# Another order by hand for layer 1 of an NSA / mLSTM step: emissions 3 to 6

## The chip, the core and the metric

The kernel runs on one core of a Trainium2 chip. The core has five engines that each take their own instructions in order: PE (the matrix unit; PEld is its weight load), DVE (vector), ACT (scalar, with the activation functions), POOL (GpSimd) and SP, which here only issues DMAs. They meet through semaphores. The metric is the device time of one execution in microseconds, the median of several runs.

## The reference

One inference step of a trunk of two layers, `x <- x + Mixer(RMSNorm(x))`, over 512 prompt tokens and 8 sample tokens, 520 columns in all, with model width 1024. Layer 0 is sparse attention (compressed, selected and window branches). Layer 1 is an mLSTM with 4 heads of width 512, and a final RMSNorm follows. Beside the outputs y the step returns the new cache rows and the new states. What matters here is layer 0's last matmul and layer 1:

```
out0  = (o * silu(z0)) @ w_out0 ;  x1 = x + out0           # 1024 x 1024
proj  = rmsnorm(x1) @ w_in                                  # 1024 -> xm 2048 | z 2048
c     = silu(conv_b + sum_j xpad[:, j:j+T] * conv_w[j])     # causal, width 4
q, k  = block-diagonal 4x4 of c ;  v = block-diagonal of xm
ig, fl = gates of concat(q, k, v) @ w_gate + b_gate
# prompt, per head: D = cumulated gates (causal), S = (q k^T) * exp(D - m)
num   = S v + decay * (q C) ; den = sum S + decay * (q n) ; h = num / max(|den|, exp(-m))
C     = carry * C + sum_s k_s w_s v_s^T                     # 512 x 512 per head
# samples: the same with one token and their own C, n, m: 8 x 4 matrices of 512 x 512
out   = (rmsnorm(h) * norm_w + skip * c) * silu(z) ;  y = x1 + out @ w_out
```

All in float32. The kernel forms a float32 product from rounded parts: an operand is split in a high half (`hhi`, `whi`, `uh`, ...: a copy in the type fp32r) and a low half (`hlo`, `wlo`, `ul`, ...: operand minus high half), and three matmuls high x high, high x low and low x high are added up.

## The kernel before, in words

Channels lie on the 128 partitions and tokens on the free axis; the 520 columns are two halves c = 0, 1 of 260. A weight tile of 128 x 1024 is loaded (`wraw`), its high half is made by a copy (`whi`, on ACT or DVE) and its low half by a subtraction (`wlo`, on DVE or POOL). Each half of an output tile takes 8 x 3 = 24 matmuls of 260 columns.

The order of the work is written out by hand. The program first records: with the recorder on, each engine call goes through `Engine.__getattr__` (line 507 issues it in the end, which is why all rows of the profile say L507) and becomes a piece of a list (`Rec`, lines 426 to 478), or an operation of a plan with its dependences (`Plan`, lines 324 to 360). Then the pieces are emitted in an order that a tuple of numbers gives, seven times:

- emissions 0 to 2 (`CALLS0`, `CALLS2`, `ORDER0`): layer 0's compression and projections, and the attention
- emission 3 (`CALLS1`, line 1956; 712 pieces, about 459 to 643.5 us): layer 0's output projection by tiles `out.ft.c` (8 tiles, 2 halves) with the addition to `x` (`x1`), the splits into `hhi` and `hlo` and the sums of squares (`sacc`, closed by a matmul with ones and the chain `rs_y`, `rv`, `rs_t`, `rr`); then layer 1's projections `xm.ft.c` of 16 tiles, convolution (`cva`), silu (`cvs`, `CT`), values (`VT`), gate products (`QKS`, `VS`) and the gates
- emission 4 (`ORDER1`, line 2312; 348 operations, to 748.3 us): the z projections of layer 1 (`zt`, `zsg`), the gates of the prompt, and head 0's state steps for the samples (`cs` in, `cs` out, 512 KB each)
- emission 5 (`ORDER2`, line 2709; 933 operations, to 997 us): for each of the 4 heads the splits of the values (`vh`, `vl`), the scores and keys (`f_po`, `f_pk`, `f_s`, `f_c`), the values (`num`), the state steps of the other heads, and the output unit with its weights (`uh`, `ul`, `x<-x,mm`)
- emission 6 (`CALLS3`, line 2760): the last part of the output, the final norm and late cache rows

The program schedules nothing of its own, so each engine's stream is its pieces in the order of the list, and the instruction at the head of a stream that waits for a semaphore holds what is behind it. SP issues its DMAs in the same way. Tiles of rotating buffers are taken in the order of the list too: a load into a buffer waits for the last reader of what was there. The `MOVED` tuples that go with the lists swap the engine of single pieces (`swapped`, lines 481 to 490): a copy by ACT goes to DVE, a copy by DVE to ACT, and a subtraction, product, addition or scalar operation from DVE to POOL or back.

Of the kernel before, what the change touches and what calls it, by code (L numbers as in the profile page):

```python
# [123 lines left out]
)  # L124
ORDER2 = (
# [42 lines left out]
)  # L168
CALLS0 = (
# [122 lines left out]
MOVED3 = (  # L292
    2, 12, 16, 23, 30, 31, 35, 42, 65, 69, 103, 120, 124, 136, 141,
)
# [249 lines left out]
def step_kernel(ctx, tc, ap):  # L544
# [1410 lines left out]
    xm_val(15)  # L1955
    R.run(NE, CALLS1, MOVED1)
    mctx.close()
# [912 lines left out]
```

## Time and profile before

| | us |
|---|---|
| median of 3 runs (lowest, highest) | 1036.99 (1036.32, 1039.83) |
| profiled execution | 1041.29 |
| its span in the trace | 1039.6 |
| PE busy in the span | 1016.4 |
| DVE, ACT, POOL busy | 790.0, 553.2, 321.7 |
| granted clock, mean | 0.995 |

The profile is of one execution. Its rows name an instruction by engine, operation and tiles (`out<-in`, buffer numbers left out), so `mm<-hhi,wlo` is a matmul of the activations' high half with a weight's low half. PE's matmuls overlap in the rows: the time that one takes is seen from start to next start (0.12 us for 260 columns in a run of them). A bracket at the end of a row gives the idle time of the engine ahead of it and what released it.

### The profile page before, as it was taken

The page shows a single profiled execution, that of the slowest core. Times are in us where ns is not written, and L with a number is a line of the kernel's source. Part 1 is how long each engine was busy: PE and PEld are TensorE (multiplying, and loading weights), DVE is VectorE, ACT ScalarE, POOL GpSimd, SP SyncE. Part 2 cuts the span into 40 slices and gives each one's busy share as a digit, 9 for nine tenths or more (in the row PEclk, how much of TensorE's full clock was granted, in tenths as well). Part 3 has the DMA queues.
Part 4 walks back from the last instruction along what each step waited for, and adds up shares of the span by engine and source line. Part 5 has one row for each costly group of instructions (what it writes and reads, how often), then busy time and mean ns, then how long its engine had stood idle before and what let it go on. Part 6 is the DMA issues. An engine that isn't in the chain of part 4 may idle for free.

```text
span 1039.6 us, 23563 instructions
## 1 busy us (share of the span) xinstructions
PE 1016.4 (98%) x8743; PEld 909.5 (87%) x8743; DVE 790.0 (76%) x1903; ACT 553.2 (53%) x1260; POOL 321.7 (31%) x374
## 2 busy tenths in 40 slices
PE   7999999999999999999999999999899999999998
PEld 6999999999998878789999998899766678877897
DVE  7856756586579988964878786775698989888985
ACT  5454344622388788632445444766455564634543
POOL 1233423331232434423331332232332234242330
PEclk9999999999999999999999999999899999999999
DMA  7654644144526344655645253788778698988543
GB/s 256 194 176 156 194 123 130 47 125 135 164 68 198 100 127 130 182 179 184 179 148 171 92 184 121 244 277 289 272 267 276 237 346 287 326 288 276 203 123 113
DMA packets 124789, 197.16 MB, mean 190 GB/s; under 512 B 16117, under 2 KB 66166, under 8 KB 124418
## 3 DMA queue, kind: packets, MB, share of 16 engines
q1 hardware_dynamic: 118866, 186.37, 55.1%
q10 hardware_dynamic: 5808, 9.28, 2.5%
q8 instruction: 69, 1.13, 0.5%
q14 instruction: 46, 0.38, 0.1%
HBM read 145.89 MB, written 58.10 MB: 196 GB/s over the span
## 4 chain that ended last, share of the span: by engine, by line
PE 79%; DVE 10%; ACT 4%; DMA 4%; issue 2%; POOL 1%; SPq 0%; DVEq 0%; ACTq 0%; POOLq 0%
PE mm L507 48%; PE s L507 17%; PE t L507 8%; PE d L507 5%; DVE cs L507 2%; ACT zsg L507 1%; DMA wc<-in_w_qkv 1%; DMA x1d<-x 1%; DVE wlo L507 1%; DVE s L507 1%; DVE hx L507 1%; DMA wraw<-in_m_in 1%; DMA praw<-in_cache 1%; ACT s L507 1%; DVE num L507 0%
## 5 line engine op out<-in xcount | busy, mean ns | idle before, releaser
L507 PE MATMUL mm<-hhi,whi 128*128 128x260 f32 (+1 forms) x952 | 273.5, 287 | 0.9 <-ACT VT L507 0.9
L507 PE MATMUL mm<-hhi,wlo 128*128 128x260 f32 (+1 forms) x952 | 270.6, 284 | 0.1
L507 PE MATMUL mm<-hlo,whi 128*128 128x260 f32 (+1 forms) x952 | 270.1, 284 | 0.0
L507 PEld LDWEIGHTS mm<-hhi,whi 128*128 128x128 f32 (+1 forms) x952 | 179.1, 188 | 5.2 <-issue 2.7
L507 PEld LDWEIGHTS mm<-hhi,wlo 128*128 128x128 f32 (+1 forms) x952 | 179.0, 188 | 0.4 <-DVE wlo L507 0.3
L507 PEld LDWEIGHTS mm<-hlo,whi 128*128 128x128 f32 (+1 forms) x952 | 178.5, 187 | 0.7
L507 POOL TENSOR_TENSOR wlo<-wraw,whi 128x1024 fp32r<-128x1024 f32 (+1 forms) x40 | 78.6, 1967 | 122.1 <-ACT whi L507 39.8
L507 ACT ACTIVATE whi<-wraw 128x1024 fp32r<-128x1024 f32 (+1 forms) x65 | 57.0, 881 | 77.0 <-PE mm L507 33.0
L507 DVE SCALAR_TENSOR_TENSOR cs<-t,wk,cs 128x512 f32<-128x512 f32 x128 | 88.7, 740 | 8.9 <-ACT cs L507 8.3
L507 ACT ACTIVATE cs<-cs,SBC 128x1024 f32<-128x1024 f32 x64 | 71.5, 1142 | 26.8 <-PE d L507 19.6
L507 DVE TENSOR_TENSOR wlo<-wraw,whi 128x1024 fp32r<-128x1024 f32 (+2 forms) x62 | 68.8, 1110 | 11.1 <-ACT whi L507 5.8
L507 PE MATMUL s<-phi,w1h 128*128 128x256 f32 (+1 forms) x256 | 75.8, 296 | 0.0
L507 PE MATMUL s<-plo,w1h 128*128 128x256 f32 (+1 forms) x256 | 74.5, 291 | 1.0 <-DVE plo L507 0.9
L507 ACT ACTIVATE s<-s,mn 128x128 f32<-128x128 f32 (+3 forms) x128 | 70.5, 555 | 6.8 <-DVE mn L507 4.8
L507 PE MATMUL s<-phi,w1l 128*128 128x256 f32 (+1 forms) x256 | 74.0, 289 | 0.0
L507 PE MATMUL mm<-uh,whi 128*128 128x260 f32 x224 | 64.5, 288 | 0.6 <-DVE x L507 0.4
L507 PE MATMUL mm<-uh,wlo 128*128 128x260 f32 x224 | 63.6, 284 | 1.1 <-DVE wlo L507 1.1
L507 DVE CUSTOM_DVE_ANT_0 s<-s,D 128x128 f32<-128x128 f32 (+3 forms) x128 | 58.5, 485 | 7.5 <-PE s L507 5.9
L507 PE MATMUL mm<-ul,whi 128*128 128x260 f32 x224 | 63.4, 283 | 0.0
L507 POOL TENSOR_SCALAR s<-s,sm 128x256 f32<-128x256 f32 (+3 forms) x47 | 42.2, 909 | 52.3 <-DVE sm L507 27.6
L507 PEld LDWEIGHTS s<-plo,w1h 128*128 128x128 f32 x256 | 48.4, 189 | 2.2 <-DVE plo L507 1.5
L507 POOL TENSOR_TENSOR plo<-praw,phi 128x1024 fp32r<-128x1024 f32 (+1 forms) x17 | 30.2, 1775 | 63.6 <-DMA praw<-in_cache 29.8
(485 smaller groups left out, 2632.2 us busy)
## 6 DMA issues: line engine op xcount, KB each, us to landing
cs<-in_state_C SPq DMA_DIRECT2D x64, 512.0 KB, 5.5
o_cs<-cs SPq DMA_DIRECT2D x64, 512.0 KB, 5.6
praw<-in_cache SPq DMA_DIRECT2D x128, 128.0 KB, 2.7
dk<-in_cache SPq DMA_DIRECT2D x128, 128.0 KB, 2.7
wraw<-in_m_in SPq DMA_DIRECT2D x32, 512.0 KB, 3.6
wraw<-in_m_out SPq DMA_DIRECT2D x32, 256.0 KB, 5.2
wraw<-in_w_kv SPq DMA_DIRECT2D x11, 512.0 KB, 4.9
wraw<-in_w_q SPq DMA_DIRECT2D x8, 512.0 KB, 3.6
```

The costliest lines, as they stand in the source:

```text
L507: return f(*[real(x) for x in a], **{n: real(x) for n, x in k.items()})
```

## The change

Four of the number tuples are replaced: the orders of emission 3 (`CALLS1`), 4 (`ORDER1`) and 5 (`ORDER2`) with their sets of swapped pieces (`MOVED1`, `MOVEDP1`, `MOVEDP2`). `CALLS3` and `MOVED3`, of emission 6, are written with other line breaks. Emissions 0 to 2 and all code outside the tuples stay as they are. The numbers index the recorded pieces, which are the same. The core of the diff, the first lines of each list (cut):

```diff
@@ ORDER1 @@
-    253, 254, 257, 225, 0, 1, 226, 2, 227, 15, 228, 229, 230, 231, 274, 232, 252, 16, 233, 30, 8, 234, 255, 256, 3,
+    0, 253, 257, 225, 226, 227, 228, 230, 1, 2, 229, 254, 15, 16, 262, 231, 232, 30, 17, 265, 233, 234, 235,
...
@@ ORDER2 @@
-    284, 315, 327, 303, 291, 286, 1, 318, 306, 290, 294, 22, 2, 402, 3, 5, 13, 7, 282, 18, 328, 307, 0, 4, 14, 295,
+    22, 282, 290, 303, 284, 402, 291, 2, 3, 1, 294, 295, 306, 315, 318, 5, 10, 7, 0, 307, 4, 13, 316, 18, 31,
...
@@ CALLS1 @@
-    44, 535, 249, 70, 28, 45, 46, 15, 0, 21, 22, 65, 64, 69, 66, 9, 4, 29, 53, 10, 30, 31, 11, 37, 12, 60, 61, 67,
+    440, 15, 0, 44, 28, 63, 1, 21, 16, 19, 4, 22, 26, 25, 70, 65, 64, 3, 9, 5, 45, 8, 6, 46, 60, 53, 2, 10, 108,
...
-MOVED1 = (
-    27, 43, 46, 52, 69, 71, 79, 86, 89, 95, 104, 105, 117, 126, 127, 147, 156, 157, 167, 169, 184, 195, 197, 212,
+MOVED1 = (20, 27, 29, 30, 36, 45, 52, 61, 62, 69, 71, 72, 73, 79, 88, 89, 95, 104, 112, 117, 126, 127, 152, 157, 164,
...
-MOVEDP1 = (
-    1, 7, 17, 22, 27, 31, 32, 37, 47, 52, 67, 76, 82, 87, 91, 112, 132, 136, 137, 142, 147, 157, 166, 182, 192, 197,
+MOVEDP1 = (7, 27, 31, 42, 46, 47, 61, 77, 82, 87, 91, 112, 117, 127, 132, 136, 162, 166, 167, 172, 177, 181, 182, 192,
...
-MOVEDP2 = (
-    94, 170, 177, 265, 283, 286, 288, 292, 295, 301, 304, 307, 313, 316, 321, 325, 327, 328, 338, 339, 347, 361,
+MOVEDP2 = (82, 94, 170, 177, 189, 265, 272, 284, 285, 286, 288, 292, 295, 309, 338, 346, 357, 362, 373, 387, 388, 389,
...
```

What the numbers mean at the places that the prediction names: in emission 3 the pieces 93 and 131 are the `hlo` splits of input tiles 5 and 7 for half 0 (41st and 42nd on DVE before, 52nd and 53rd after), 142 is the addition of the last output half (45th before, 49th after), 148 is the matmul that sums its squares (20th and 18th on PE), and 174 is the low half of the second xm weight (43rd and 62nd on DVE). In emission 4 operation 2 is the low half of the first z weight (2nd and 4th on DVE, counted from 0), 227 the first gate bias. In emission 5 operations 286 and 288 are value splits (high halves) on DVE, 289 a low half on POOL, and 300 the first product of values and keys, which comes 20th on PE before and 14th after.

More of the change, by code (lines that the diff above doesn't have):

```diff
@@ L246 @@
 CALLS1 = (
[32 rows of a table removed]
-)
-MOVED1 = (
[6 rows of a table removed]
-)
[33 rows of a table added]
+)
+MOVED1 = (20, 27, 29, 30, 36, 45, 52, 61, 62, 69, 71, 72, 73, 79, 88, 89, 95, 104, 112, 117, 126, 127, 152, 157, 164,
[6 rows of a table added]
 MOVED2 = (
@@ L291 @@
 )
-MOVED3 = (
-    2, 12, 16, 23, 30, 31, 35, 42, 65, 69, 103, 120, 124, 136, 141,
-)
+MOVED3 = (2, 12, 16, 23, 30, 31, 35, 42, 65, 69, 103, 120, 124, 136, 141,)
 MOVEDP0 = (
@@ L301 @@
 )
-MOVEDP1 = (
-    1, 7, 17, 22, 27, 31, 32, 37, 47, 52, 67, 76, 82, 87, 91, 112, 132, 136, 137, 142, 147, 157, 166, 182, 192, 197,
-    202, 207, 211, 217, 225, 230, 255,
-)
-MOVEDP2 = (
[5 rows of a table removed]
-)
+MOVEDP1 = (7, 27, 31, 42, 46, 47, 61, 77, 82, 87, 91, 112, 117, 127, 132, 136, 162, 166, 167, 172, 177, 181, 182, 192,
+    196, 197, 202, 211, 212, 248, 255,)
+MOVEDP2 = (82, 94, 170, 177, 189, 265, 272, 284, 285, 286, 288, 292, 295, 309, 338, 346, 357, 362, 373, 387, 388, 389,
[5 rows of a table added]
 LATE = ((3, 1), (3, 2), (3, 3))
```

208 rows, old and new, of tables (CALLS1, CALLS3, MOVED1, MOVEDP2) are left out of this document.

## The prediction

> **What bounds the kernel now.** I read the page's engine table first, then the chain of waits, the stretches of the three emissions whose lists differ, and last the matmul engine's waits.
>
> ```profile
> span 1039.6 us, 23563 instructions
> PE 1016.4 (98%) x8743; PEld 909.5 (87%) x8743; DVE 790.0 (76%) x1903; ACT 553.2 (53%) x1260; POOL 321.7 (31%) x374
> PE 79%; DVE 10%; ACT 4%; DMA 4%; issue 2%; POOL 1%; SPq 0%; DVEq 0%; ACTq 0%; POOLq 0%
> ```
>
> PE is busy 98% of the span and holds 79% of the chain that ended last. The order of PE's own work hardly matters to its length; what matters is whether each operand is there when PE comes to it. The table by stretch (columns: the stretch, then busy time and number of instructions on PE, PEld, DVE, ACT, POOL, the granted clock, the DMA share and GB/s) has emission 3 at 459 to 643.5 us, emission 4 up to 748.3, emission 5 up to 997 and emission 6 behind it:
>
> ```profile
> 459.00:643.50 184.50, 182.17 (x1576) 177.68 (x1572) 130.63 (x282) 82.89 (x181) 58.49 (x72) 0.99 0.47 152
> 643.50:748.30 104.80, 101.87 (x861) 93.74 (x858) 72.80 (x128) 64.92 (x123) 32.30 (x41) 0.99 0.79 271
> 748.30:997.00 248.70, 245.18 (x1729) 186.77 (x1728) 220.26 (x479) 130.02 (x218) 74.83 (x81) 0.99 0.81 274
> ```
>
> PE is idle for 184.50 - 182.17 = 2.33 us, 2.93 us and 3.52 us: 8.8 us in the 538 us that the change touches. The waits of PE over the whole span, and the one place where a wait has an after-effect:
>
> ```profile
> PE t L507 <- DVE pr L507: 2.9, 1, 2.9
> PE mm L507 <- DVE wlo L507: 2.5, 3, 1.4
> ...
> 747.01 0.34 PE L507 MATMUL t<-pr,ones 128*32 128x32 f32 x8 [2.91 <-DVE pr L507]
> 747.28 1.12 PE L507 MATMUL t<-cst,lse 128*128 128x128 f32 x4
> 748.19 5.20 PE L507 MATMUL mm<-CT,bdm 128*128 128x512 f32 x6
> 753.22 0.60 PE L507 MATMUL t<-cst,VS 128*8 128x128 f32 x4
> ...
> 756.18 1.02 PE L507 MATMUL mm<-CT,bdm 128*128 128x512 f32 x2
> ```
>
> After the wait of 2.91 us, six matmuls of 512 columns took about 5.1 us from start to next start (748.19 to 753.22), 0.84 us each; the same matmul at 756.18 goes at 1.02 / 2 = 0.51 at most. So that wait costs its 2.9 us and 2 us more (6 x 0.33). A list that fed PE without a gap could win 8.8 + 2 = 10.8 us at the very most; what a worse one can lose has no such limit.
>
> **The change, part by part.** The diff replaces the order of emission 3 (712 recorded pieces), of emission 4 (348) and of emission 5 (933), and the sets of instructions whose engine is swapped there. List 6 holds the same numbers in the same order before and after, with other line breaks: its stretch changes by nothing of its own. No instruction is added or removed in the other three; counted in the two lists, 3 to 6% of the pairs on each of PE, DVE and ACT stand the other way round, up to 17% on POOL and on SP, the DMA queue. In emission 3, 45 instructions go from DVE to POOL and 35 back, 33 from ACT to DVE and 28 back. In emission 5 it is 46 and 27, and 22 and 24. So PE's sum of work stays, and the cost is the sum of the places where an operand comes late. I followed the new lists by hand at the borders of the stages, where buffers and engines have least lead, with durations of the trace.
>
> *Start of emission 3.* One of the three waits for a weight's low half is here:
>
> ```profile
> 461.59 0.35 SPq L507 DMA_DIRECT2D scr<-in_state_conv  x1
> ...
> 473.89 1.77 DVE L507 TENSOR_TENSOR wlo<-wraw,whi 128x1024 fp32r<-128x1024 f32 x1
> ...
> 475.71 0.39 PE L507 MATMUL mm<-uo,wlo 128*128 128x260 f32 x1 [1.40 <-DVE wlo L507]
> ```
>
> The SP queue opens at 461.59, when the buffers of the stage ahead come free. The new list puts the weights of output tile 2 earlier behind that point, so the 1.40 us should go; but the weights of tile 3, issued ahead of the block in the old list, now stand behind it, and ahead of the later loads stands a store of x1 that waits for a DVE addition. Term: -1.4, with +2.0 as the other end (the DVE step of 1.77 us, late a second time). I take -1.4, since tile 3 is asked for one tile (2 x 2.9 us of PE) later.
>
> *From the output tiles to layer 1's projection.* Here the list moves most:
>
> ```profile
> 507.64 0.47 PE L507 MATMUL mm<-hhi,whi 128*128 128x260 f32 x1
> ...
> 509.76 0.28 PE L507 MATMUL mm<-hlo,whi 128*128 128x260 f32 x1
> ...
> 510.48 0.28 PE L507 MATMUL mm<-hlo,whi 128*128 128x260 f32 x1
> ```
>
> ```profile
> 506.26 2.08 DVE L507 SCALAR_TENSOR_TENSOR hlo<-x,nw,hhi 128x260 fp32r<-128x260 f32 x5
> 508.69 1.23 DVE L507 TENSOR_TENSOR wlo<-wraw,whi 128x1024 fp32r<-128x1024 f32 x1 [0.34 <-ACT whi L507]
> ...
> 510.73 0.41 DVE L507 TENSOR_TENSOR x<-x,mm 128x260 f32<-128x260 f32 x1
> ```
>
> PE starts the first layer-1 projection at 507.64 and takes the low halves of input tiles 0 to 7 in turn, three matmuls apart: tile 5 at 509.76 and tile 7 at 510.48. In the old list the five splits at 506.26 made the last of these just ahead of PE. In the new one the splits of tiles 5 and 7 follow the addition of the last output half (the row at 510.73) and two other splits. PE finished that half at about 507.4 (the projection follows it without a gap), so the addition lies between 507.9 and, where it lay in before, 510.73; tile 7's split ends 0.41 + 4 x 0.42 = 2.1 us after its start, at 510.0 to 512.8. The second sum of squares, which the new list puts on PE right behind this projection (before, two projections later), needs one more addition of 0.42 us on the same engine and shares the wait. Ends: 0 and 512.8 - 510.48 = 2.3; since the work set ahead of the addition on DVE grows by 3.0 us (counted from the lists with the durations of before), up to 5.3. I take **+2.0**: DVE was 3 us behind here already.
>
> The low half of the next weight (508.69, 1.23 us) falls behind eight further DVE steps, some 3.4 us, the last of which scales the first projection's result. That gives 510.0 + 0.4 + 3.4 + 1.2 = 515.0 to 517.8, plus whatever the chain through ACT's square root adds, about 0.8 in before. PE has two projections and the small sum ahead of it: 507.6 + 2.9 + 0.6 + 2.9 = 514.0, plus the wait just taken. Term **+1.4** (0 to 2.9, one projection).
>
> *Start of emission 4.* The next low half in line is behind more on DVE:
>
> ```profile
> 645.04 1.99 PE L507 MATMUL t<-gs,cst 128*128 128x260 f32 x8
> ...
> 647.11 0.28 PE L507 MATMUL mm<-hhi,wlo 128*128 128x260 f32 x1
> ```
>
> ```profile
> 644.02 1.22 DVE L507 TENSOR_TENSOR wlo<-wraw,whi 128x1024 fp32r<-128x1024 f32 x1
> 645.78 0.49 DVE L507 TENSOR_SCALAR gi<-t,bg 128x260 f32<-128x260 f32 x1 [0.53 <-PE t L507]
> ```
>
> The new list puts it behind the first gate bias, which needs the matmuls at 645.04, and behind a copy that comes over from ACT (0.4): 645.78 + 0.49 + 0.4 + 1.22 = 647.9 where PE asks at 647.11, 0.8 late; the matmul that feeds the bias is moved 0.6 us ahead, which leaves 0.2. Term **+0.5** (0 to 1.0). The low halves of the next two tiles go to POOL, which has nothing there, and PE asks for them 10 us and more later: nothing, and 1 us each if POOL were busy.
>
> *End of emission 4.* The chain to the 2.91 us wait keeps its members and nearly its places: 0.
>
> *Start of emission 5.*
>
> ```profile
> 750.61 0.28 DVE L507 TENSOR_TENSOR bdm<-cst,mw 128x128 f32<-128x128 f32 x1
> ...
> 756.74 0.29 DVE L507 TENSOR_TENSOR bdk<-cst,wc 128x128 f32<-128x128 f32 x1
> ...
> 758.88 1.22 DVE L507 TENSOR_TENSOR bdk<-cst,wc 128x128 f32<-128x128 f32 x1
> ```
>
> ```profile
> 758.67 2.56 POOL L507 TENSOR_TENSOR vl<-VT,vh 128x512 fp32r<-128x512 f32 x2 [11.40 <-ACT vh L507]
> ```
>
> ```profile
> 771.14 0.48 PE L507 MATMUL mm<-vh,kwh 128*128 128x512 f32 x1
> ```
>
> The first values-times-keys product moves on PE from 20.4 to 13.5 us of work behind the start, so it is asked for at 771.14 - 6.9 = 764.2. DVE, free from the head's closing chain at 750.6, has 13.3 us ahead of the last split for it, then POOL one of 1.28: 765.2. Term **+1.0** (-1.0 to +3.0; below nothing if the half-clock matmuls come away).
>
> *The swaps and the other places.* What a swap costs in length, emission 5, POOL then DVE (busy us, mean ns of one, then idle time before):
>
> ```profile
> L507 POOL TENSOR_TENSOR wlo<-wraw,whi 128x512 fp32r<-128x512 f32 x12 | 16.0, 1331 | 36.3 <-PE mm L507 16.0 <-ACT whi L507 11.6 <-DVE whi L507 5.3
> L507 POOL TENSOR_TENSOR ul<-num,uh 128x512 fp32r<-128x512 f32 x7 | 9.9, 1421 | 14.4 <-ACT uh L507 5.8 <-DVE uh L507 4.6 <-PE mm L507 4.0
> ```
>
> ```profile
> L507 DVE TENSOR_TENSOR wlo<-wraw,whi 128x512 fp32r<-128x512 f32 x12 | 8.2, 681 | 0.4 <-ACT rs_y L507 0.4
> L507 DVE TENSOR_TENSOR ul<-num,uh 128x512 fp32r<-128x512 f32 x6 | 4.1, 683 | 0.0
> ```
>
> ```profile
> L507 POOL TENSOR_TENSOR wlo<-wraw,whi 128x1024 fp32r<-128x1024 f32 (+1 forms) x40 | 78.6, 1967 | 122.1 <-ACT whi L507 39.8
> ...
> L507 DVE TENSOR_TENSOR wlo<-wraw,whi 128x1024 fp32r<-128x1024 f32 (+2 forms) x62 | 68.8, 1110 | 11.1 <-ACT whi L507 5.8
> ```
>
> The last two are the whole span's, 40 and 62 low halves of weights. A result made on POOL comes 0.65 to 0.74 us later. In emissions 3 and 5, 45 + 46 = 91 results get this; a move behind one more DVE step costs as much. If one in twelve of the 91 is asked for by PE inside that time, that is 7.6 x 0.7 = 5 us. The rate is my choice: in before 3 of the 102 weight low halves of both engines kept PE waiting, and my five places were found in some 110 of 538 us. Ends: -4.5, the idle time that is left to win (8.8 - 1.4 - 2.9), and +15, the POOL time that emission 5 gains by the lists (a net 19 instructions more, large and small, 0.8 us each on the mean). I take **+5**.
>
> Sum: -1.4 + 2.0 + 1.4 + 0.5 + 1.0 + 5 = **+8.5 us**; the ends add to -6.9 and +29.2. The profiled execution took 1041.29 us, 1.7 more than its span and 4.3 more than the median of 1036.99 (runs 1036.32 to 1039.83), so it would come to about 1049.8, and the median to 1036.99 + 8.5, about **1045**.
>
> **A rule weighed.** The last DVE rows above show one DVE product of 0.29 us taking 1.22 beside POOL's two of 1.28: DVE loses 0.93 us to 1.28 of POOL. The Trainium skill ("SBUF — State Buffer", Who interferes with whom) has a rule for this: a DVE instruction with two SBUF inputs and a POOL instruction that reads SBUF exclude each other, and the later one waits for the whole instruction. The trace agrees at this place. By the rule the relief of DVE in the next part would be eaten up, as the POOL time added blocks DVE in its turn, and the faster rival would shrink to the 1.4 us of the first wait; by the rows of single instructions alone it stands.
>
> **The rivals.** *No measurable change.* PE's leads are long inside the stages (DVE is idle 248.7 - 220.3 = 28 us in emission 5, 54 in emission 3), so the places I found merge and the rest costs nothing: -1.4 + 2.0 + 1.4 = +2, time 1039. Against it: three borders come short by hand at once.
>
> *Much slower.* The waits chain: DVE gets a step that waits for POOL, everything behind it on DVE stands, and PE's pauses reach the length of the one at 747, after which the next 5 us run at half speed. Four such pauses at 2.9 + 2 us are +20, with the sum above +28: time 1065. For it, DVE has hardly a gap behind the start of emission 5 (third figure of the row):
>
> ```profile
> 760.00:780.00 20.00, 19.94 (x141) 13.65 (x139) 19.07 (x37) 10.18 (x18) 6.79 (x10) 1.00 0.76 247
> ```
>
> Against it: only one pause of that length in 538 us of before.
>
> *Faster.* In emission 5 DVE loses 19 instructions net to POOL, at 0.6 us each 11 us of 220. If DVE's backlog is what causes the small waits of PE, they go along with the 1.40 at 475: -1.4 - 4.5 = -6, time 1031. It decides only if nothing at the borders comes late; against it stands that PE's whole idle time in emission 5 is 3.5 us.
>
> *The change does less than it says.* For list 6 this is so, by the diff; for the other three the places differ.
>
> **How the numbers follow.** Chances: the forecast (4 to 18 us slower) 0.62, much slower 0.17, no measurable change 0.13, faster 0.08. A measurement of this kernel tells 0.3% (3.1 us) from no change: slower 0.79, within it 0.13, faster 0.08. The range takes the unmeasurable case's lower edge, 1035, and on the other side most of the much slower case, 1063; the forecast's own range is 1041 to 1055.
>
> **What would show it.** Right: PE's busy time stays near 1016 and its idle time grows by 8 us; the wait at 475 for a low half is gone; a wait of PE for hlo or sacc of about 2 us shows where the first layer-1 projection begins, another for a low half some 8 us on, one of under a microsecond at the gates' start; in emission 5 waits for values made on POOL (ul, vl, wlo). By stretch: +2.0 in emission 3, +0.5 in 4, +1 in 5, and the 5 of the rest mostly in 3 and 5. Wrong: if the three stretches keep 184.5, 104.8 and 248.7 us; if the loss sits in emission 4, where least is swapped; if it comes from DMA waits, which I cost at nothing beyond the start; or if emission 5 becomes shorter, which would mean DVE's load and not its order is what PE waits for.

## The result, and the profile after

The changed kernel takes 1031.48 us (median of 7 runs, 1030.38 to 1033.42) where the kernel before takes 1036.99 (7 runs beside them, 1034.99 to 1039.83): a ratio of 0.9947, 95% interval 0.9930 to 0.9963. So it is 5.5 us faster (3.8 to 7.3), where 8.5 us slower was forecast. The profiled execution took 1030.38 us. From the page of the changed kernel, engines and chain:

```profile
span 1028.6 us, 23534 instructions
PE 1010.4 (98%) x8743; PEld 907.0 (88%) x8743; DVE 780.3 (76%) x1881; ACT 545.7 (53%) x1254; POOL 345.7 (34%) x402
...
PE 88%; DVE 5%; ACT 2%; DMA 2%; issue 1%; POOL 1%; SPq 0%; ACTq 0%; DVEq 0%; POOLq 0%
```

PE does the same 8743 matmuls; its share of the chain rose from 79 to 88%, DVE's fell from 10 to 5. POOL has 24 us more work and DVE 10 us less, as the lists say. Between the two profiles PE's idle time falls from 23.2 to 18.2 us and its busy time from 1016.4 to 1010.4. The busy time of these same matmuls isn't a constant: it is 1012.0 us in the repeated kernel before (below), in part because some matmuls behind a wait go at half speed in one execution and not in another (last section). The stretches of emissions 3, 4 and 5 of the changed kernel (columns as in the table before):

```profile
458.10:638.30 180.20, 179.96 (x1570) 176.01 (x1572) 132.46 (x276) 76.88 (x176) 65.33 (x82) 1.00 0.47 157
638.30:742.20 103.90, 101.73 (x861) 92.76 (x854) 73.26 (x133) 62.75 (x119) 33.58 (x39) 1.00 0.79 277
742.20:986.10 243.90, 241.75 (x1736) 186.81 (x1729) 209.21 (x457) 129.99 (x219) 90.02 (x102) 0.99 0.83 280
```

Against 184.5, 104.8 and 248.7 these are shorter by 4.3, 0.9 and 4.8 us. That is more than the times allow for, because the profile of before was of a long execution (1041.29 us against a median of 1036.99). The stretch of an emission in which nothing was changed, from PE's first matmul of it to the first of the next, is in the profiles of before and of the runs below 181.6 to 184.2 us (mean of 9: 183.0) for emission 3, 104.2 to 104.9 (mean of 10: 104.5) for 4 and 245.0 to 248.9 (mean of 8: 246.4) for 5. Against these means the new lists save 2.7 us (mean of 3), 0.8 (of 2) and 3.2 (of 2), 6.7 together. The three stretches of the changed kernel itself add up to 528.0 us against 533.9 of the means, 5.9 less, which fits the 5.5 measured.

The longest of PE's waits in the changed kernel behind its start (columns: us in total, times, longest; a line of 0.6 us of the attention is left out):

```profile
PE t L505 <- DVE pr L505: 2.0, 1, 2.0
PE mm L505 <- DVE wlo L505: 1.5, 1, 1.5
PE s L505 <- DVE mn L505: 0.9, 2, 0.7
...
PE mm L505 <- POOL Sl L505: 0.6, 1, 0.6
```

The wait at 475 for a low half is gone, as is the one for VT (0.9); none over 0.15 us has come at the three borders where the prediction set one. For the largest of these, DVE and PE in the changed kernel:

```profile
504.70 0.42 DVE L505 TENSOR_TENSOR x<-x,mm 128x260 f32<-128x260 f32 x1 [1.00 <-PE mm L505]
505.04 1.68 DVE L505 SCALAR_TENSOR_TENSOR hlo<-x,nw,hhi 128x260 fp32r<-128x260 f32 x4
...
509.60 1.22 DVE L505 TENSOR_TENSOR wlo<-wraw,whi 128x1024 fp32r<-128x1024 f32 x1
```

```profile
504.75 0.47 PE L505 MATMUL mm<-hhi,whi 128*128 128x260 f32 x1
...
507.59 0.28 PE L505 MATMUL mm<-hlo,whi 128*128 128x260 f32 x1
```

The addition of the last output half runs as soon as PE lets it, after DVE has stood idle for 1.00 us; in before it ran 3 us late. The four splits behind it are done at 506.72, and PE takes the last low half at 507.59 without a gap.

### The profile page after: what moved, and what is told of

Same layout as the page of the kernel before. It is cut to its first block, busy times and chain, and to the rows that moved or that the text cites. A ratio compares the mean times of both kernels' runs of the same rounds, so it can differ in the third digit from the quotient of the medians.

```text
span 1028.6 us, 23534 instructions
## 1 busy us (share of the span) xinstructions
PE 1010.4 (98%) x8743; PEld 907.0 (88%) x8743; DVE 780.3 (76%) x1881; ACT 545.7 (53%) x1254; POOL 345.7 (34%) x402
## 4 chain that ended last, share of the span: by engine, by line
PE 88%; DVE 5%; ACT 2%; DMA 2%; issue 1%; POOL 1%; SPq 0%; ACTq 0%; DVEq 0%; POOLq 0%
PE mm L505 54%; PE s L505 19%; PE t L505 10%; PE d L505 6%; DMA wraw<-in_m_in 1%; DVE num L505 1%; ACT zsg L505 1%; DMA wraw<-in_m_out 1%; DVE s L505 1%; ACT s L505 1%; DMA x_t<-in_xT 0%; DVE ul L505 0%; DVE x L505 0%; POOL wlo L505 0%; DVE sc L505 0%
## 5 line engine op out<-in xcount | busy, mean ns | idle before, releaser
L505 POOL TENSOR_TENSOR wlo<-wraw,whi 128x1024 fp32r<-128x1024 f32 (+1 forms) x45 | 85.8, 1907 | 128.2 <-DVE whi L505 65.8
L505 DVE TENSOR_TENSOR wlo<-wraw,whi 128x1024 fp32r<-128x1024 f32 (+2 forms) x57 | 64.6, 1135 | 11.2 <-ACT whi L505 5.8
L505 ACT ACTIVATE whi<-wraw 128x1024 fp32r<-128x1024 f32 (+2 forms) x54 | 46.7, 869 | 40.2 <-PE mm L505 14.8
## 6 DMA issues: line engine op xcount, KB each, us to landing
wraw<-in_m_out SPq DMA_DIRECT2D x32, 256.0 KB, 4.9
```

Of the source, the lines that this page charges most:

```text
L505: return f(*[real(x) for x in a], **{n: real(x) for n, x in k.items()})
```

## The experiments

The theories. **Places**: each emission loses short waits of its own. **Load** (first called DVE relief): the gain is DVE's work that went to POOL. **Fit**: order and engine choice of a list belong together, and neither has a price by itself. The last was put up only when the run with the new order and the old swaps of emission 5 was known, in which both theories on record had missed. Ratios are to the kernel before, with 95% intervals; "us" beside them is the ratio's distance from 1 times 1036.6.

**Each emission alone.** The lists of one emission are the new ones.

```diff
 em3:  CALLS1, MOVED1    old -> new
 em4:  ORDER1, MOVEDP1   old -> new
 em5:  ORDER2, MOVEDP2   old -> new
```

> Order and swaps of emission 3 alone are the new ones. Places theory (each emission loses its own small waits of the matmul engine, independently): the stretch of emission 3 falls from 184.2 us to about 180.3, as in the profile of the changed kernel, emissions 4 and 5 keep 104.7 and 248.9, and the time falls by 2 to 4 us. DVE-relief theory (the gain comes from work that left DVE in emission 5): no more than 1 us.

> Emission 4 alone is new. Places theory: its stretch falls from 104.7 to about 103.9, the wait for the product pr from 2.9 to about 2.0, and the time by 0 to 1 us. The prediction's term for this stage, +0.5 us at the gates' start, would show as a wait there for a weight's low half.

> Emission 5 alone is new, order and swaps. Places theory: its stretch falls from 248.9 to about 244, the time by 2 to 5 us. DVE-relief theory: the same, with all of the gain of 5.5 us here. With em3 and em4 the three changes add up to that of the changed kernel within 1.5 us.

Measured: 0.9964 (0.9953 to 0.9975) for emission 3, 0.9979 (0.9968 to 0.9991) for 4, 0.9964 (0.9950 to 0.9979) for 5: -3.7, -2.2 and -3.7 us. Their stretches are 180.1, 103.6 and 242.6 us. So every list is better than the old one, and half of the gain is not in emission 5. The three add up to -9.6 us where the whole change gives -5.5; that is a miss of the expectation for their sum, and emission 4 alone gained more than its stretch and than the 0 to 1 us expected. Part of the difference shows in the profiles: the new list of emission 5 takes 243.9 us in the changed kernel and 242.6 alone, and 1.3 us of that are matmuls at half speed at its start, of which the profiles of the three single kernels have none (last section). Whether the medians differ for this reason isn't shown. The stretches also act on each other: behind the new list of emission 3 the old list of emission 4 takes 105.2 to 105.4 us in three runs instead of 104.5. That makes emission 3 alone look smaller, so it doesn't explain a sum that is too large.

**The same kernel again.**

```diff
 MOVED3 = (
+
     2, 12, 16, 23, ...
```

> The kernel before with one line break more, nothing else. Every theory: no change, within 0.1%, stretches of emissions 3, 4 and 5 at about 183.5, 104.5 and 245 to 249 us. It shows by how much a stretch differs from run to run when nothing in it has changed, and so how much of the difference of the two first profiles is the change.

Measured: 1.0003 (0.9993 to 1.0014). The comparison is sound to 0.1%. Its stretches, 181.6, 104.9 and 247.3 us, are among those counted above.

**Order without swaps.** Emission 5 in the new order; then the old swaps in full, in one half and in the other; and emission 3 in the new order with the old swaps.

```diff
 em5_order:  ORDER2 old -> new ; MOVEDP2 old
 em5_pool:   ORDER2 old -> new ; MOVEDP2: only the 73 DVE <-> POOL entries new
 em5_copy:   ORDER2 old -> new ; MOVEDP2: only the 46 ACT <-> DVE copies new
 em3_order:  CALLS1 old -> new ; MOVED1 old
```

> Emission 5 has the new order with the old set of swapped instructions, so DVE keeps its load of about 220 us in that stretch. DVE-relief theory: the gain of emission 5 is gone, the time is that of before within 1 us. Order theory (what counts is that the heads of DVE's and PE's queues wait less, whichever engine does the work): at least half of the gain of the kernel with emission 5 alone stays.

> Emission 5 in the new order; the 73 swaps between DVE and POOL are the new ones, the 46 of copies between ACT and DVE are the old ones. Load theory (the new order holds if DVE has about 10 us less work): DVE is busy for about 210 us of the stretch and most of the gain of 3 us stays, time 1033 to 1036. Fit theory (order and engine of each single piece belong together; any piece on the other engine stands at a wrong place in a queue): 10 us slower than before or more.

> The other half: new order, the 46 swaps of copies new, the 73 between DVE and POOL old. Load theory: DVE keeps about 220 us of work, the time is that of the new order with all the old swaps, about 1065. Fit theory: between 1040 and 1060, each half of the swaps having its own misplaced pieces.

> Emission 3 in the new order with the old set of swaps; emissions 4 and 5 as before. There DVE is busy for 131 of 184 us, so load theory: it has room, and the gain of 3.4 us stays within 1 us. Fit theory: the gain is lost and the time is above that of before by 3 us or more, as in emission 5.

Measured: 1.0277 (1.0259 to 1.0295), 1.0124 (1.0109 to 1.0140), 1.0174 (1.0158 to 1.0191) and 0.9993 (0.9983 to 1.0004): +28.7, +12.9, +18.0 and -0.7 us. The stretch of emission 5 in the runs with all swaps new (the kernel with emission 5 alone), none, only those with POOL, only the copies:

```profile
745.30:987.90 242.60, 240.50 (x1731) 186.63 (x1730) 208.84 (x458) 130.00 (x219) 89.53 (x99) 1.00 0.82 281
```

```profile
746.00:1024.50 278.50, 255.97 (x1729) 193.35 (x1728) 225.40 (x479) 129.89 (x218) 73.89 (x81) 0.96 0.71 244
```

```profile
744.90:1006.00 261.10, 248.95 (x1731) 190.05 (x1729) 215.56 (x460) 129.28 (x217) 90.23 (x98) 0.98 0.76 261
```

```profile
745.70:1011.70 266.00, 252.08 (x1730) 192.14 (x1728) 225.24 (x477) 130.87 (x220) 73.92 (x81) 0.97 0.75 256
```

Load falls. With the POOL swaps DVE has 215.6 us of work in 261 and the kernel is 13 us slow; in the repeated kernel before it had 220.3 in 247.3 and was not. And emission 3 gained with more work on DVE (132.5 us against 130.6). Either half of the swaps put on the wrong engine costs 16 to 22 us against the kernel with both, more than the whole gain. In emission 3, where DVE has 50 us to spare, the order alone is worth nothing that can be told. The expectation by load was wrong in both places. By fit a loss of 3 us or more had been expected in emission 3 too, and none came. The loss of 28.7 us with the order alone in emission 5 had been expected by no theory. What the missing swaps do is seen in the longest new wait of the run with all old swaps:

```profile
PE s L507 <- DVE q L507: 5.8, 2, 4.9
```

A copy of q, 0.6 to 0.7 us long on either engine, keeps PE waiting for 4.9 us. Idle time is not all of it: between the first two of the four rows PE's busy time grows by 15.5 us (240.5 to 256.0) for the same matmuls and its idle time by 20.4, while the granted clock of the stretch falls from 1.00 to 0.96 (the second profile is of a long execution, 1069.08 us against a median of 1065.53). What a wait costs is thus also paid in slow matmuls behind it.

**One piece.** Emission 5 new, and one copy of q back on DVE; then, instead of it, two subtractions Sl back from POOL to DVE.

```diff
 em5_q:   MOVEDP2 = new with 535 added
 em5_sl:  MOVEDP2 = new without 477, 820
```

> Emission 5 new in order and swaps, but for one piece: the copy of q for head 2, first tile, goes back from ACT to DVE. As one instruction of about 0.6 us on either engine it should cost nothing by its length (price theory of the prediction: 0.1 us). Fit theory: on DVE it stands behind other work at that place of the list, PE waits for it 2 to 5 us, and the kernel is 2 to 6 us slower than the one with emission 5 new, that is 1035 to 1040.

> Emission 5 new, but for two subtractions Sl (head 1 third block, head 3 second block) that go back from POOL to DVE, where one takes 0.4 to 0.6 us less. Price theory of the prediction (POOL's results come later by its longer time): the same or up to 1 us faster than the kernel with emission 5 new. Fit theory: both come later, by 2 us each and more, since DVE's queue is ahead of them; 3 to 5 us slower, 1036 to 1039.

Measured: 0.9995 (0.9981 to 1.0008), which is 3.2 us more than the kernel with emission 5 new, and 0.9988 (0.9976 to 1.0000), 2.5 us more (here the two intervals overlap a little; 3 to 5 us had been expected). For the copy, DVE and PE of that run:

```profile
826.85 0.68 DVE L508 TENSOR_TENSOR num<-num,hy 128x512 f32<-128x512 f32 x1
827.57 0.75 DVE L508 SCALAR_TENSOR_TENSOR num<-CT,par,num 128x512 f32<-128x512 f32 x1
828.23 0.68 DVE L508 COPY q<-mm 128x512 f32<-128x512 f32 x1
```

```profile
825.61 1.47 PE L508 MATMUL d<-cs,QZ 128*32 128x512 f32 x12
828.97 3.27 PE L508 MATMUL s<-q,CT 128*128 128x512 f32 x5 [1.89 <-DVE q L508]
```

In the kernel with emission 5 new the copy ran on ACT (the last row of ACT for q) and PE went on without a gap:

```profile
823.43 0.60 ACT L508 ACTIVATE q<-mm 128x512 f32<-128x512 f32 x1
```

```profile
822.56 1.91 PE L508 MATMUL d<-cs,QZ 128*32 128x512 f32 x16
824.40 4.58 PE L508 MATMUL s<-q,CT 128*128 128x512 f32 x16
```

On DVE it stands behind the products num; PE waits 1.89 us, and the first six matmuls behind the wait take 3.50 us from start to start instead of 2.04, some 1.4 us more. Together this is 3.3 us, about what was measured. (The profile is of a long execution, 1039.23 us against a median of 1035.98, and holds other losses too.) One entry of `MOVEDP2` thus eats nearly the whole gain of the emission. For Sl the faster engine made it worse: against their neighbours in POOL's queue the two pieces end some 3.7 and 3.5 us later than in the kernel with emission 5 new. The named waits are smaller than expected, though:

```profile
PE mm L508 <- POOL Sl L508: 1.1, 1, 1.1
PE s L508 <- DVE mn L508: 0.9, 2, 0.7
...
PE mm L508 <- DVE Sl L508: 0.8, 2, 0.6
```

The two pieces themselves keep PE waiting for 0.8 us (last row). Where the rest of those 2.5 us lies isn't settled. In the profile, 1.4 us of the longer stretch come from slow matmuls behind the wait for pr, which that of emission 5 alone doesn't have (below); they stand ahead of the moved pieces.

**Emission 3, swaps without order, and a single wait of the order alone.**

```diff
 em3_swap:  MOVED1 old -> new ; CALLS1 old
 em3_ct:    CALLS1 old -> new ; MOVED1 = old without 632, 651
```

> Emission 3 in the old order with the new set of swaps. Fit theory: the gain of 3.4 us is lost, and PE gets new waits; slower than before by 0 to 5 us. Load theory (the swaps relieve ACT by 5 us and put 10 us on POOL, and this is the gain): the gain stays at 2 us or more.

> Emission 3 in the new order with the old swaps, but for two products CT (tiles 14 and 15), which go from POOL to DVE as in the new set. In the run with the new order alone PE waited 1.0 us for CT on POOL at the end of this stage. Fit theory: that wait goes, the stretch of emission 3 falls from 182.1 to about 180.8 and the time by 1.3 us against the new order alone, to about 1035.

Measured: 1.0038 (1.0024 to 1.0052), +3.9 us, and 0.9988 (0.9976 to 1.0000), no different from the order alone. So in emission 3 the swaps alone cost 3.9 us, the order alone gives nothing that can be told, and both together save 3.7. With the swaps alone PE waits for low halves on POOL and DVE:

```profile
PE mm L508 <- POOL wlo L508: 2.0, 2, 1.1
PE mm L508 <- DVE wlo L508: 1.4, 2, 1.2
```

The second run missed: the 1.0 us that PE waited for CT on POOL became 0.4 for CT on DVE, and the stretch was 183.3 instead of the 180.8 expected. These two products by themselves are not what the order alone lacks.

**The prediction's largest border term, by itself.** Only the two splits are moved, in the list of before.

```diff
-    ... 113, 50, 131, 93, 174, 40, 135, 137, 142, 146, 110, ...
+    ... 113, 50, 174, 40, 135, 137, 142, 93, 131, 146, 110, ...
```

> The kernel before with only one of the differences: the low-half splits of input tiles 5 and 7 go behind the addition of the last output half on DVE, as in the changed list; all else stays. Old-surroundings theory (the prediction's term was right for a DVE queue as late as that of before, and failed because the new list has DVE on time there): the addition still comes about 3 us after its matmuls, the splits end some 0.8 us behind it, and PE waits about 1 us for a low half in the first layer-1 projection; the stretch of emission 3 grows by 1 us. If the addition comes early here too, there is no wait, and the term was wrong in itself.

Measured: 0.9995 (0.9982 to 1.0009) in time, which can't tell 1 us, and neither can the stretch (183.5 us, among unchanged ones of 181.6 to 184.2); in the trace the wait is there. DVE, then PE:

```profile
508.11 0.41 DVE L507 TENSOR_TENSOR x<-x,mm 128x260 f32<-128x260 f32 x1
508.45 0.88 DVE L507 SCALAR_TENSOR_TENSOR hlo<-x,nw,hhi 128x260 fp32r<-128x260 f32 x2
```

```profile
508.98 0.39 PE L507 MATMUL mm<-hlo,whi 128*128 128x260 f32 x1 [1.65 <-DVE hlo L507]
```

The addition comes 3.1 us behind its matmuls (they end where the projection begins, at 505.0), the splits follow, and PE waits 1.65 us where 1 had been expected; the first projection takes 5.0 us from its start to the next one's instead of 3.1 in before. So the term's arithmetic held for a DVE queue as late as that of before.

**A better list?** The changed kernel, and two of its waits attacked where they stand.

```diff
 ORDER1
-    ... 219, 220, 216, 217, 336, 337, 221, 222, 223, 338, 339, 346, ...
+    ... 219, 220, 216, 217, 336, 337, 338, 339, 221, 222, 223, 346, ...
 ORDER2
-    ... 237, 916, 907, 866, 855, 867, 856, 917, 911, ...
+    ... 237, 916, 907, 917, 866, 855, 867, 856, 911, ...
```

> The changed kernel with four pieces at other places of their lists, chosen from its own waits: in emission 4 the last z gate (its sigmoid, product and copy) behind the denominator's steps of the closing head, in emission 5 the low half of one output weight ahead of the last products num on DVE. If the waits are head-of-queue waits, the one for pr falls from 2.0 to about 1.2 and the one of 1.5 for the low half goes: 2.3 us less, and up to 2 us more if the matmuls after the shorter wait are no longer at half speed: 1027 to 1030. If the time is set elsewhere, the waits return at the next place and the time is that of the changed kernel, 1031.5.

Measured: 0.9944 (0.9927 to 0.9962), the same as the changed kernel. Its waits:

```profile
PE t L509 <- POOL bdk L509: 1.7, 1, 1.7
PE t L509 <- DVE pr L509: 1.3, 1, 1.3
PE mm L509 <- POOL bdm L509: 1.0, 1, 1.0
```

The wait for pr fell from 2.0 to 1.3 as expected and the one of 1.5 for the low half went; in their places PE waits 1.0 us for bdm and 1.7 us for bdk, both on POOL. The wait for bdm stands a few instructions behind that for pr, the one for bdk 4 us behind the place of the low half. The time that was freed came back as waits at the next places.

## Why the prediction was wrong, point by point

**What bounds the kernel**: right. PE is busy 98% before and after, and the gain of 5.5 us stays inside the 10.8 that the prediction gave as the most that could be won. The reservoir was in short waits and the slow matmuls behind them, and was used to a half.

**Start of emission 3, -1.4**: right. The part up to the first layer-1 projection takes 46.6 us in all five runs with the new order and 46.7 to 48.3 (mean 47.7) in the others: 1.1 us on the mean, 1.7 against the profile from which the term was read.

**Output tiles to layer 1, +2.0, and the next weight, +1.4**: wrong, 0 both. The step that failed is that the addition was placed "where it lay in before", with the 3.0 us of work set ahead of it added on top. The run with only the two splits moved shows the wait (1.65 us); in the changed list the queue it was charged to is empty. The same stretch, up to the first projection, in the repeated kernel before and in the changed one (behind the length stand the busy times of PE, PEld, DVE, ACT and POOL):

```profile
457.20:504.40 47.20, 46.86 (x387) 46.65 (x386) 26.12 (x46) 14.83 (x32) 15.73 (x15) 1.00 0.53 176
```

```profile
458.10:504.70 46.60, 46.60 (x387) 46.58 (x386) 32.45 (x54) 12.99 (x31) 15.42 (x15) 1.00 0.57 187
```

DVE does 32.5 us of work there instead of 26.1: what stands "ahead" in the new list fills time in which DVE stood waiting for PE in the old one. One such wait of the kernel before:

```profile
487.33 0.43 DVE L507 TENSOR_TENSOR x<-x,mm 128x260 f32<-128x260 f32 x1 [5.00 <-PE mm L507]
```

The prediction counted the work that moved ahead and not the idle time that it moved into, though the trace shows both. It had the other end, 0, among its bounds and chose against it.

**Start of emission 4, +0.5**: nearly. The low half was made at 640.96 to 642.18 and PE took it at 642.24, about 0.1 us late. **Start of emission 5, +1.0**: wrong, 0; PE took the product at 758.45, 16.3 us behind the start, without a gap.

**The swaps and the other places, +5**: wrong in sign, and this is the term that carried the forecast. It priced a swap by the longer time on POOL (0.65 to 0.74 us) and took one in twelve to reach PE. With the border terms as they came (-1.1, 0, 0, +0.1, 0), about -4.5 us of the measured -5.5 are left for this term, which is its lower end: nearly all the idle time that it counted as left to win. The pieces that were tried show that the length has little to do with the cost. Two subtractions moved to the faster engine made the kernel some 2.5 us slower, one copy of about equal length on either engine 3.2 us slower: a piece comes when its place in its engine's queue comes, and the place was chosen with the engine. In emission 3 the swaps cost 3.9 us without their order; in emission 5 the order costs 28.7 us without its swaps. In the sum of a prediction that prices both separately these would be losses, and together they are a gain.

**The rivals.** The faster one gave 1031, and 1031.48 was measured, but its mechanism is not what the runs show, so the hit was luck. It set the gain in emission 5, in DVE's smaller load; emission 5 has about half of it, and a run with DVE's load 5 us below that of before (215.6 us) lost 13. The prediction named a shorter emission 5 as a sign that DVE's load is what PE waits for. The sign came and did not mean that. The mechanism of the much slower one, an in-order queue in which one misplaced piece holds up those behind it, is real, as the run with the old swaps shows; it just isn't in a list whose places and engines were made for one another. The relief of DVE was not eaten up, as it would be by the rule that the prediction weighed: in emission 5 POOL has 15 us more work, and DVE is busy for 209.2 us instead of 220.3. The Trainium skill ("SBUF — State Buffer", Who interferes with whom) says that a DVE instruction with two SBUF inputs and a POOL instruction that reads SBUF contend; that rule did not decide here.

**Open.** It isn't settled why the three emissions add up to 9.6 us one by one and give 5.5 together, beyond the 1.3 us seen in the profiles of emission 5. The swaps of emission 5 without their order were not tried. The new orders also move the loads on SP; what these are worth was not separated from the order on the engines, nor was each of the many small waits that went followed to its cause.

## What to carry to other kernels

An order by hand and the choice of engines that goes with it are one schedule: price neither by itself, and do not value a place of the new list with the queues of the old trace. Before charging for work that moves ahead of an instruction, look for the idle time of that engine ahead of it in the same stretch (here 47.2 - 26.1 = 21 us); work that falls into it need not delay anything. Idle time in the sum is no guarantee, though: in emission 3 DVE is idle for 54 us, and the new swaps in the old order still cost 3.9. Where PE is busy for 98%, what is left to win here are waits of up to 3 us, most of them under 1, and removing one of them may only uncover the next.

## What the runs showed of the hardware

The prediction took the slow matmuls behind the 2.91 us wait as a fixed 2 us. They are not fixed. The same lists up to the wait, and the same wait, in the run with emission 5 alone:

```profile
744.64 0.27 PE L508 MATMUL t<-pr,ones 128*32 128x32 f32 x8 [2.91 <-DVE pr L508]
...
745.76 2.74 PE L508 MATMUL mm<-CT,bdm 128*128 128x512 f32 x6
```

Six matmuls of 512 columns in 2.74 us, at full speed from the first, where before's profile had 5.20 us. The granted clock of the 12 us from the first of these matmuls on is 1.00 there and 0.79 in before. Over the 16 profiles, with waits of 1.3 to 2.9 us, between 0 and 5 of these six matmuls went at about 0.85 us from start to start instead of 0.43: none in the run with the two splits moved, which has the old lists of emissions 4 and 5, two in the repeated kernel before. In the changed kernel with four pieces moved some did behind waits of only 1.33 and 1.03 us:

```profile
741.50 0.27 PE L509 MATMUL t<-pr,ones 128*32 128x32 f32 x8 [1.33 <-DVE pr L509]
741.70 0.60 PE L509 MATMUL t<-cst,VS 128*8 128x128 f32 x4
743.32 3.19 PE L509 MATMUL mm<-CT,bdm 128*128 128x512 f32 x4 [1.03 <-POOL bdm L509]
```

That up to 2.1 us come and go like this from run to run can be part of why times of one kernel spread by 4 to 7 us; that was not measured by itself. The Trainium skill ("TensorE: Matmul & The Clock Gate", What's actually happening) says that PE's activity is judged in a window that runs freely and doesn't start with the kernel, so that the moment of the change varies from run to run. The variation agrees with it; the window itself is in no trace here.
